# The prologue of the running streams' stage rebuilt, and the first norm done by thirds

## The chip, the cores and the metric

The kernel runs on one core of a Trainium2 chip. A core has a matrix engine (TensorE, PE in the profile), a vector engine (VectorE, DVE), an activation engine (ScalarE, ACT), a general engine (GpSimd, POOL) and a queue engine (SyncE, SP) that issues most transfers. Each engine works through its own instructions in order. The metric is the device time of one execution in microseconds, the median of several runs. Lower is better.

## The reference, cut to what matters

One layer of a streaming encoder is computed for two groups at once: one new stream of 16 + 1024 rows, and 8 running streams of 16 new rows each with a cache of 272 rows. All numbers are float32.

```python
u = rms_norm(h, g_mix)
q, k, v, z, xbc, dt_raw, gate_logits = split(u @ w_in)
att = stick_breaking(q, k, v)              # new stream: its own keys
                                           # running streams: cached keys, then the new ones
ssd = ssd_mix(xbc, z, dt_raw, ...)         # conv, chunked scan, gated norm per group
merged = gate_att * (att @ w_br_att) + gate_ssd * (ssd @ w_br_ssd)
h = h + merged @ w_out
u = rms_norm(h, g_ffn)
h = h + (silu(gate) * val) @ w_down        # gate, val = split(causal_dwconv(u @ w_up))

def stick_breaking(q, k, v):               # per head; reach: key before query
    z = q @ k.T * 64 ** -0.5
    beta = where(reach, sigmoid(z), 0)
    w = beta * (product over later keys of (1 - beta))
    return w @ v
```

Outputs are the final rows of both groups and the new keys, values and states.

## The kernel before, in words

Precision: every large product is done three times, on a high part and a low part of each operand. `split` makes them: a cast on ScalarE (L97) and a subtraction on VectorE (L98). Weights are loaded and split in `weights` (L104 to L106); `mm3` issues the products of one output tile, high by high (L115), low by high (L118), high by low (L119), for each of 8 blocks of the inner dimension. One output block of 128 columns is three tiles of rows (384, 384 and 386 or 400), so 72 matmuls.

Stages in order of the program (`body`):

1. `norm_in`: the rows come in 10 blocks (`x`, L238), handled in three thirds of 3, 3 and 4 blocks. For each block ScalarE squares and sums (L241), takes a root (L242), VectorE makes the reciprocal and refines it (L244, L174 to L177), builds a diagonal (L248), and TensorE spreads it over partitions into `rb` (L249). TensorE transposes the rows (`tp`, L135), ScalarE copies them to `xt` (L264), and VectorE scales them (`un`, L270), after which `split` writes the normalized input `u`, kept in the pool `slotA`. `xt` also goes out to `s_xT` (L276).
2. `phase_ssd`: the state-space part of all four groups.
3. `phase_att`: 16 heads of the new stream. A head loads its keys, queries and values, makes scores (`z`, L721 and L724), a sigmoid (L684), the running product by a scan on VectorE (L688, L690), transposes (`wT`), splits, and the value products (`o`, L745, L746, L753) in two halves `g` of four row blocks. Between the heads stand fill blocks: the remaining q, k, v projections and 16 gate blocks (`gate`, L672, stored by L673). `paced` takes fill blocks from a list; each of a block's three tiles is ordered behind a mark, one of the score matmuls of the heads.
4. `phase_smp`: first `first_queries` (L763 to L802), the first two rows of the new stream for all heads, a small computation that borrows the buffers `Ksh`, `Vsh` and `last`; then `sample_att`, the running streams' attention, 8 streams in two halves of 8 heads each; then `norm_rows` (L926 to L931), which turns the sums of squares of the state-space part (`s_ss`) into factors (`s_rs`). `sample_att` begins with a prologue: queries `qhs`, `qls` (L810), new keys into `kxh`, `kxl` beside the 16 last cached ones (16 loads, L815), the cached rows themselves (16 loads, L821), transposed and split, and the diagonal query tiles `qdh`, `qdl` (L832). In the loop each half loads cached keys and values (`ck`, L856, L858), copies the last keys into `Ksh`, `Ksl` on GpSimd (L862), and does scores (L881 to L885), sigmoid, scan, transposes, and value products (L904 to L906). The output collects in `aout` and is stored once at the end (L918). Six gate blocks are paced by this loop.
5. `phase_merge`: `RESERVE` = 3 gate blocks come first, then `br_ssd`, whose moving operands `ssd_operands` makes: a factor row `rB` (L938), then per block a load `yt` (L941), a multiplication (L943), and the high and low part (L944, L945). Operands 0 to 7 go to the pool `slotB`, 8 to 15 to `slotA`, which is free once the gates no longer read `u`.
6. `phase_ffn`.

What sets the order: a planner orders the instructions of each engine ahead of time by its own estimate of their durations and by the order of the program; at run time each engine keeps that order. Pools open and close like a stack, and a pool opened after another has closed takes its bytes; a tile on such bytes waits for the old tiles that it overlaps, not for the whole stage. Within a stage the order in which pools are named sets which old tile lies under which new one.

## Time and profile before

| | |
|---|---|
| median of 3 runs | 2992.92 us (2991.86 to 2997.25) |
| the profiled execution, its own time | 2993.68 us |
| its span | 2991.6 us |
| PE busy | 2915.2 us, 97% of the span |
| DVE, ACT, POOL busy | 1711.6, 1263.0, 610.3 us |
| first norm | about 0 to 65 us |
| last head ends, running streams begin | about 1445 to 1490 us |
| running streams end, merge begins | about 1645 to 1740 us |

The page lists engines by busy time. A row of the groups reads: line, engine, operation, tile written from tiles read, shapes, count, then busy time and mean duration in ns, then the idle time before it and what ended it. In a row in order of time the first number is the start, the second the duration in us, and the brackets hold the idle time before it and the releaser. The granted clock is that of TensorE, 1.00 being full speed.

### The profile page before, as it was taken

How to read it: one execution, taken by the hardware profiler on the slowest of the kernel's cores; microseconds unless marked ns; L12 is line 12 of the kernel's file. 1: busy time of each engine (PE TensorE's matmuls, PEld its weight loads, DVE VectorE, ACT ScalarE, POOL GpSimd, SP SyncE). 2: the span in 40 equal slices, each digit the busy share in tenths (PEclk: the TensorE clock that was granted, in tenths of full speed). 3: DMA queues.
4: the chain of work that ended last, by engine and by line, in shares of the span. 5: the costliest groups of instructions: out<-in, count | busy, mean ns of one | idle time of the engine just before them, and what ended most of it. 6: DMA issues, size and time to landing. Idle time of an engine off the chain costs nothing. (4 is left out here: it accounts for less than half of the span.)

```text
span 2991.6 us, 45527 instructions
## 1 busy us (share of the span) xinstructions
PE 2915.2 (97%) x17399; PEld 2766.0 (92%) x17399; DVE 1711.6 (57%) x2625; ACT 1263.0 (42%) x2630; POOL 610.3 (20%) x964
## 2 busy tenths in 40 slices
PE   7999999999999999999799899999999999999998
PEld 5998988989889999999789899999999999999998
DVE  6457666576657778777544431446755454545447
ACT  6345454454445455444344310214534242424245
POOL 0023142231322233333233000003201010101013
PEclk9999999999999999999899999999999999999999
DMA  5435355353575555543444643546211111111113
GB/s 187 115 86 157 112 149 147 99 151 108 161 220 145 166 134 144 145 129 98 101 133 131 191 146 98 159 108 185 65 51 44 39 42 43 44 44 37 43 44 120
DMA packets 445496, 338.44 MB, mean 113 GB/s; under 512 B 43991, under 2 KB 421155, under 8 KB 445279
## 3 DMA queue, kind: packets, MB, share of 16 engines
q1 hardware_dynamic: 444063, 333.77, 39.2%
q8 instruction: 137, 2.24, 0.3%
q10 hardware_dynamic: 1216, 1.77, 0.2%
q14 instruction: 80, 0.66, 0.1%
HBM read 244.31 MB, written 91.15 MB: 112 GB/s over the span
## 5 line engine op out<-in xcount | busy, mean ns | idle before, releaser
L115 PE MATMUL mm<-sh,wh 128*128 128x384 f32 (+3 forms) x2520 | 868.3, 346 | 10.3 <-ACT sh L944 5.2
L118 PE MATMUL mm<-sl,wh 128*128 128x384 f32 (+3 forms) x2520 | 869.9, 345 | 1.4 <-DVE sl L98 1.1
L119 PE MATMUL mm<-sh,wl 128*128 128x384 f32 (+3 forms) x2520 | 864.7, 343 | 0.0
L115 PEld LDWEIGHTS mm<-sh,wh 128*128 128x128 f32 (+1 forms) x2520 | 474.5, 188 | 23.6 <-ACT sh L944 5.8
L118 PEld LDWEIGHTS mm<-sl,wh 128*128 128x128 f32 (+1 forms) x2520 | 474.9, 188 | 15.6 <-issue 10.3
L119 PEld LDWEIGHTS mm<-sh,wl 128*128 128x128 f32 (+1 forms) x2520 | 474.9, 188 | 9.4 <-issue 7.8
L115 PE MATMUL mm<-ph,wh 128*128 128x386 f32 x1248 | 424.7, 340 | 0.7 <-DVE st L1041 0.7
L118 PE MATMUL mm<-pl,wh 128*128 128x386 f32 x1248 | 424.9, 340 | 0.0
L106 DVE TENSOR_TENSOR wl<-wf,wh 128x1024 fp32r<-128x1024 f32 (+2 forms) x205 | 253.4, 1237 | 297.5 <-ACT wh L105 281.2
L119 PE MATMUL mm<-ph,wl 128*128 128x386 f32 x1248 | 422.7, 339 | 0.2 <-DVE wl L106 0.2
L105 ACT CAST wh<-wf 128x1024 fp32r<-128x1024 f32 (+2 forms) x205 | 212.5, 1037 | 480.4 <-PE mm L118 455.8
L1153 DVE SCALAR_TENSOR_TENSOR acc<-fx,cwf,acc 128x384 f32<-128x384 f32 (+1 forms) x352 | 170.8, 515 | 155.5 <-ACT acc L1151 151.7
L115 PEld LDWEIGHTS mm<-ph,wh 128*128 128x128 f32 x1248 | 236.3, 189 | 1.6 <-DVE st L1041 1.0
L119 PEld LDWEIGHTS mm<-ph,wl 128*128 128x128 f32 x1248 | 236.2, 189 | 1.1 <-DVE wl L106 0.7
L118 PEld LDWEIGHTS mm<-pl,wh 128*128 128x128 f32 x1248 | 235.2, 188 | 1.7
L688 DVE TENSOR_TENSOR_SCAN keep<-keep 128x144 f32<-128x144 f32 (+7 forms) x128 | 180.0, 1409 | 54.0 <-POOL keep L687 53.4
L115 PE MATMUL mm<-ah,wh 128*128 128x384 f32 x528 | 179.7, 340 | 0.0
L119 PE MATMUL mm<-ah,wl 128*128 128x384 f32 x528 | 179.2, 339 | 0.0
L118 PE MATMUL mm<-al,wh 128*128 128x384 f32 x528 | 179.0, 339 | 0.0
L1080 POOL TENSOR_TENSOR sq<-sq,sq 128x386 f32<-128x386 f32 (+1 forms) x39 | 57.6, 1477 | 463.4 <-ACT sq L1079 455.5
L1178 DVE TENSOR_TENSOR h<-mm,h 128x384 f32<-128x384 f32 x144 | 79.7, 555 | 120.0 <-PE mm L119 119.5
L98 DVE TENSOR_TENSOR wTl<-wT,wTh 128x512 fp32r<-128x512 f32 (+3 forms) x176 | 103.0, 601 | 79.1 <-ACT wTh L97 78.2
(329 smaller groups left out, 4523.9 us busy)
## 6 DMA issues: line engine op xcount, KB each, us to landing
wf<-in_w_in SPq DMA_DIRECT2D x80, 512.0 KB
wf<-in_w_up SPq DMA_DIRECT2D x44, 512.0 KB
t<-s_ac SPq DMA_DIRECT2D x36, 512.0 KB
wf<-in_w_down SPq DMA_DIRECT2D x28, 512.0 KB
wf<-in_w_out SPq DMA_DIRECT2D x24, 512.0 KB
s_y<-x SPq DMA_DIRECT2D x16, 577.0 KB
yt<-s_y SPq DMA_DIRECT2D x16, 577.0 KB
KH<-s_kh SPq DMA_DIRECT2D x32, 260.0 KB
```

The source lines that it names most:

```text
L98: nc.vector.tensor_tensor(out=l, in0=x, in1=h.bitcast(F32), op=ALU.subtract)
L105: nc.scalar.copy(wh, wf)
L106: nc.vector.tensor_tensor(out=wl, in0=wf, in1=wh.bitcast(F32), op=ALU.subtract)
L115: i = nc.tensor.matmul(p, wh[:, k, :], mh[:, c:c + w], start=s, stop=False)
L118: nc.tensor.matmul(p, wh[:, k, :], ml[:, c:c + w], start=False, stop=False)
L119: nc.tensor.matmul(p, wl[:, k, :], mh[:, c:c + w], start=False, stop=e)
L688: nc.vector.tensor_tensor_scan(out=K[:, ::-1], data0=K[:, ::-1], data1=K[:, ::-1], initial=1.0, op0=ALU.mult, op1=ALU.min)
L1080: nc.gpsimd.tensor_tensor(out=acc[:, :w], in0=acc[:, :w], in1=sq, op=ALU.add)
L1153: nc.vector.scalar_tensor_tensor(out=op, in0=src(q), scalar=w(q), in1=op, op0=ALU.mult, op1=ALU.add)
L1178: self.nc.vector.tensor_tensor(out=h, in0=p, in1=h, op=ALU.add)
```

## The change

- The first norm: the sums of squares of a third share one tile; root, reciprocal and refinement are done once per third. Blocks 1 and 2 are loaded by ScalarE's queue. `x` has 6 buffers instead of 5, `xt` holds 2 blocks of columns instead of 4 (so four stores per third instead of two), `rB` has 1 buffer, `un` 3. For two of eight column blocks GpSimd does both halves of the split.
- The attention pools: the heads' tiles get one name for even and one for odd heads with one buffer each (two before under one name), and the pools of both attention stages, and of the fill and row tiles, are opened in another order.
- `first_queries` is called ahead of the last head, and takes its buffers from the pool `cache`, which is opened after the second head.
- The cached rows 256 to 271 of all streams are copied into a scratch tensor `s_ck` after the second head, and loaded from it by two loads. New keys come by two loads into their own tiles; the loop copies the two pieces of 16 keys separately.
- `norm_rows` is called ahead of `sample_att`.
- After the last head one more gate block is taken from the list, ordered behind the last score mark and behind the first value product of each half of the last head. `RESERVE` is 2 instead of 3. The running streams keep six gate blocks.

The diff, cut to its core:

```diff
-RESERVE = 3
+RESERVE = 2
...
+        self.s_ck = dr([TS, 1024], 's_ck')
...
             for p0, p1, c0 in ((0, 3, 0), (3, 6, 384), (6, 10, 768)):
                 xn, o = [], 0
                 rb = self.tile(ps, [128, 512], F32, 'rb', bufs=1)
+                np_ = p1 - p0
+                s = self.tile(sp, [128, 2, 4], F32, 'ss')
+                if p1 == 10:
+                    nc.gpsimd.memset(s[:, 0, 0:np_], 1.0)
                 for i in range(p0, p1):
                     n = sizes[i]
-                    x = self.tile(sp, [128, D], F32, 'x', bufs=5)
+                    x = self.tile(sp, [128, D], F32, 'x', bufs=6)
                     for r, e, src in rows[i]:
-                        nc.sync.dma_start(x[r:e], src)
-                    s = self.tile(sp, [128, 2], F32, 'ss', bufs=4)
+                        (nc.scalar if i in (1, 2) else nc.sync).dma_start(x[r:e], src)
                     sq = self.tile(ps, [128, D], F32, 'sq', bufs=1)
-                    nc.scalar.activation(sq[:n], x[:n], AF.Square, accum_out=s[:n, 0:1])
-                    root = nc.scalar.activation(s[:n, 1:2], s[:n, 0:1], AF.Sqrt, bias=self.eps[:n], scale=1.0 / D)
-                    r = self.tile(sp, [128, 1], F32, 'rs', bufs=4)
-                    nc.vector.reciprocal(r[:n], s[:n, 1:2])
-                    self.refine(sp, r[:n], s[:n, 0:1], 1.0 / D)
+                    nc.scalar.activation(sq[:n], x[:n], AF.Square, accum_out=s[:n, 0, i - p0:i - p0 + 1])
+                    xn.append((x, n))
+                root = nc.scalar.activation(s[:, 1, :np_], s[:, 0, :np_], AF.Sqrt, bias=self.eps, scale=1.0 / D)
+                r = self.tile(sp, [128, 4], F32, 'rs')[:, :np_]
+                nc.vector.reciprocal(r, s[:, 1, :np_])
+                self.refine(sp, r, s[:, 0, :np_], 1.0 / D)
+                for i, (x, n) in enumerate(xn):
...
-                    nc.vector.tensor_scalar(out=dg[:n, :n], in0=self.ident[:n, :n], scalar1=r[:n], scalar2=None, op0=ALU.mult)
+                    nc.vector.tensor_scalar(out=dg[:n, :n], in0=self.ident[:n, :n], scalar1=r[:n, i:i + 1], scalar2=None,
+                                            op0=ALU.mult)
                     nc.tensor.matmul(rb[:, o:o + n], self.ones[:n], dg[:n, :n], start=True, stop=True)
-                    xn.append((x, n))
                     o += n
...
-                xt = [self.tile(sp, [128, 4, 400], F32, 'xt', bufs=3) for _ in range(2)]
+                xt = [self.tile(sp, [128, 2, 400], F32, 'xt', bufs=5) for _ in range(4)]
...
-                    nc.scalar.copy(xt[k // 4][:, k % 4, :w], p[:, :w])
-                rB = self.tile(sp, [128, 400], F32, 'rB', bufs=2)
+                    nc.scalar.copy(xt[k // 2][:, k % 2, :w], p[:, :w])
+                rB = self.tile(sp, [128, 400], F32, 'rB', bufs=1)
...
                 for k in range(8):
-                    y = self.tile(sp, [128, 400], F32, 'un', bufs=2)[:, :w]
-                    nc.vector.scalar_tensor_tensor(out=y, in0=xt[k // 4][:, k % 4, :w], scalar=gT[:, k:k + 1], in1=rB[:, :w],
+                    y = self.tile(sp, [128, 400], F32, 'un', bufs=3)[:, :w]
+                    nc.vector.scalar_tensor_tensor(out=y, in0=xt[k // 2][:, k % 2, :w], scalar=gT[:, k:k + 1], in1=rB[:, :w],
                                                    op0=ALU.mult, op1=ALU.mult)
                     uh, ul = self.u[k]
-                    self.split(uh[:, c0:c0 + w], ul[:, c0:c0 + w], y)
-                    if k % 4 == 3:
-                        q = k // 4
-                        nc.sync.dma_start(self.s_xT[512 * q:512 * q + 512, c0 + z - T0:c0 + w - T0]
+                    uh, ul = uh[:, c0:c0 + w], ul[:, c0:c0 + w]
+                    if k in (2, 5):
+                        nc.gpsimd.tensor_copy(uh, y)
+                        nc.gpsimd.tensor_tensor(out=ul, in0=y, in1=uh.bitcast(F32), op=ALU.subtract)
+                    else:
+                        self.split(uh, ul, y)
+                    if k % 2 == 1:
+                        q = k // 2
+                        nc.sync.dma_start(self.s_xT[256 * q:256 * q + 256, c0 + z - T0:c0 + w - T0]
                                           .rearrange("(i p) t -> p i t", p=128), xt[q][:, :, z:w])
...
-        KH, KL = (self.tile(ap, [128, TP], F32R, n) for n in ('KH', 'KL'))
-        QS = self.tile(ap, [128, TP - T0], F32R, 'QS')
-        VV = self.tile(ap, [128, 9, 128], F32R, 'VV')
+        KH, KL = (self.tile(ap, [128, TP], F32R, f'{n}{h % 2}', bufs=1) for n in ('KH', 'KL'))
+        QS = self.tile(ap, [128, TP - T0], F32R, f'QS{h % 2}', bufs=1)
+        VV = self.tile(ap, [128, 9, 128], F32R, f'VV{h % 2}', bufs=1)
...
-                nc.tensor.matmul(po[:, lo:], VV[:, j, :], wh[:, lo:], start=(j == 0), stop=False)
+                mm = nc.tensor.matmul(po[:, lo:], VV[:, j, :], wh[:, lo:], start=(j == 0), stop=False)
+                if j == 0:
+                    self.pv_marks = [mm] if g == 0 else self.pv_marks + [mm]
...
-        x = self.tile(ap, [128, 4, 288], F32R, 'Ksh').bitcast(F32).rearrange("p a b -> p (a b)")[:, :288]
-        x = x.rearrange("p (i j t) -> p i j t", i=2, j=8)
+        x, v, Q = (self.tile(self.ckp, [128, 2, 512], F32, 'ck').rearrange("p a b -> p (a b)") for _ in range(3))
+        x = x[:, :288].rearrange("p (i j t) -> p i j t", i=2, j=8)
...
-        v = self.tile(ap, [128, 2, 512], F32R, 'Vsh').bitcast(F32)[:16].rearrange("p a (j c) -> p (a j) c", c=128)
+        v = v[:16].rearrange("p (j c) -> p j c", c=128)
...
-        Q = self.tile(ap, [128, 512], F32, 'last', bufs=2)[:, :256].rearrange("p (j c) -> p j c", c=32)
+        Q = Q[:, :256].rearrange("p (j c) -> p j c", c=32)
...
-        ps = self.tile(pa, [128, 512], F32, 'z')
+        ps = self.tile(pa, [128, 512], F32, 'z', bufs=2)
...
-        po = self.tile(pa, [128, 512], F32, 'o')
+        po = self.tile(pa, [128, 512], F32, 'o', bufs=2)
...
-        kx = [self.tile(ap, [128, 8, NB, 32], F32R, n, bufs=1) for n in ('kxh', 'kxl')]
-        for j in range(8):
-            for t, src in zip(kx, (self.s_kh, self.s_kl)):
-                nc.sync.dma_start(t[:, j, :, 16:32].bitcast(F32),
-                                  src[128 * j:128 * j + 128, TP:T].rearrange("p (b t) -> p b t", t=16))
+        kc, kn = ([self.tile(ap, [128, 8, TS], F32R, n + x, bufs=1) for x in 'hl'] for n in ('kc', 'kn'))
+        for t, src in zip(kn, (self.s_kh, self.s_kl)):
+            nc.sync.dma_start(t.bitcast(F32), src[:, TP:T].rearrange("(j p) t -> p j t", p=128))
         for hf in range(2):
             lk = self.tile(ap, [128, 512], F32, 'last', bufs=2)
-            ck = a['cache_k'][0].rearrange("b s h d -> b s (h d)")
-            for b in range(NB):
-                nc.sync.dma_start(lk[16 * b:16 * b + 16], ck[b, 256:272, 512 * hf:512 * hf + 512])
+            nc.sync.dma_start(lk, self.s_ck[:, 512 * hf:512 * hf + 512])
...
-            v = pk.rearrange("p (j b s) -> p j b s", j=4, s=16)
-            h, l = (t[:, 4 * hf:4 * hf + 4, :, 0:16] for t in kx)
-            for j in range(4):
-                self.split(h[:, j], l[:, j], v[:, j])
+            self.split(*(t[:, 4 * hf:4 * hf + 4] for t in kc), pk.rearrange("p (j s) -> p j s", j=4))
...
-                    nc.gpsimd.tensor_copy(K[:, :, 256:288], kx[x][:, 4 * hf:4 * hf + 4, b].bitcast(F32))
+                    for i, k in enumerate((kc, kn)):
+                        nc.gpsimd.tensor_copy(K[:, :, 256 + 16 * i:272 + 16 * i],
+                                              k[x][:, 4 * hf:4 * hf + 4, 16 * b:16 * b + 16].bitcast(F32))
...
             self.ap = {n: self.pool(c1, "att_" + n, 2) for n in (
-                'wTh', 'wTl', 'wf32', 'att', 'vf', 'KH', 'KL', 'QS', 'VV', 'keep', *(f'beta{i}' for i in range(8)))}
+                'KH0', 'KL0', 'QS0', 'VV0', 'vf', *(f'beta{i}' for i in range(8)), 'KH1', 'KL1', 'QS1', 'VV1', 'keep',
+                'wTh', 'wTl', 'wf32', 'att', 'fb', 'fw', 'fo')}
...
                 for e in range(2):
+                    if p == 7 and e == 1:
+                        self.first_queries()
                     marks += self.head(2 * p + e, v[:, :, 64 * e:64 * e + 64])
...
-        self.ckp = self.pool(right, "cache", 4, side='right')
+                        self.ckp = self.pool(right, "cache", 4, side='right')
+                        self.nc.sync.dma_start(self.s_ck.rearrange("(b s) c -> b s c", s=16),
+                                               self.a['cache_k'][0, :, 256:272].rearrange("b s h d -> b s (h d)"))
+            self.fill.pop(0)([marks[-1]] + self.pv_marks)
...
         with ExitStack() as c2:
-            mp = self.stp = self.pool(c2, "mixst", 3)
+
             self.ap = {n: self.pool(c2, "smpa_" + n, 2) for n in (
-                'aout', 'od', 'wTh', 'wTl', 'keep', 'beta', 'v', 'r', 'newton', 'qdh0', 'qhs', 'qls', 'kxh', 'kxl',
-                'last', 'V3h', 'V3l', 'qdl0', 'qdh1', 'qdl1', 'Ksh', 'Ksl', 'Vsh', 'Vsl',
-                'w30', 'w31', 'fb', 'fw', 'fo')}
+                'last', 'qdh0', 'qdl0', 'qdh1', 'qdl1', 'qhs', 'qls', 'knh', 'knl', 'kch', 'kcl', 'Ksh', 'Ksl', 'V3h', 'V3l',
+                'v', 'r', 'newton', 'beta', 'keep', 'Vsh', 'Vsl', 'w30', 'w31', 'wTh', 'wTl', 'od', 'aout')}
+            self.stp = self.pool(c2, "mixst", 3)
             self.pa = self.pool(c2, "smp_ps", 1, space=PSUM)
             rest, self.fill = self.fill[len(self.fill) - RESERVE:], self.fill[:len(self.fill) - RESERVE]
-            self.first_queries()
+            self.norm_rows(self.ap)
             self.sample_att(3 * len(self.fill) / 16)
-            self.norm_rows(self.ap)
...
             with ExitStack() as c1:
+                k.rowp = k.pool(c1, "rows", 2)
                 k.stp = k.pool(c1, "fill", 7)
-                k.rowp = k.pool(c1, "rows", 2)
```

## The prediction

> **What bounds the kernel now.** I read the page first, then a table of stretches, then the TensorE (PE) order of time where the table shows holes, then the queues that release PE there.
>
> ```profile
> span 2991.6 us, 45527 instructions
> ...
> PE 2915.2 (97%) x17399; PEld 2766.0 (92%) x17399; DVE 1711.6 (57%) x2625; ACT 1263.0 (42%) x2630; POOL 610.3 (20%) x964
> ```
>
> PE is busy for 97% of the span, so the bound is matmul work and the question is where PE stands still or runs slowly. The change adds and removes almost no matmul work, so I count in "lost time": the length of a stretch less busy time times granted clock. The columns are stretch, its length, busy time of PE, weight loads, DVE, ACT, POOL, the clock, the DMA share and GB/s.
>
> ```profile
> 6.00:20.00 14.00, 10.22 (x43) 7.31 (x43) 9.38 (x39) 12.09 (x29) 0.38 (x2) 1.00 0.96 311
> 20.00:65.00 45.00, 38.41 (x190) 27.52 (x191) 29.74 (x79) 29.84 (x70) 0.00 (x0) 0.89 0.44 150
> 1445.00:1465.00 20.00, 13.17 (x59) 9.58 (x58) 11.71 (x15) 6.25 (x14) 4.59 (x8) 0.74 0.89 111
> 1465.00:1490.00 25.00, 17.03 (x93) 16.09 (x92) 8.10 (x23) 10.27 (x23) 7.68 (x17) 0.66 0.56 154
> 1645.00:1660.00 15.00, 10.06 (x49) 6.81 (x49) 5.26 (x10) 6.78 (x13) 1.96 (x3) 1.00 0.24 69
> 1700.00:1712.00 12.00, 7.92 (x30) 7.09 (x30) 6.61 (x5) 3.84 (x4) 0.00 (x0) 0.72 0.70 224
> 1712.00:1740.00 28.00, 26.58 (x151) 26.26 (x150) 18.61 (x14) 9.35 (x8) 0.00 (x0) 1.00 0.69 224
> 1750.00:1800.00 50.00, 50.00 (x287) 50.00 (x286) 10.88 (x15) 5.25 (x5) 0.00 (x0) 1.00 0.42 127
> ```
>
> The first norm (6 to 65) loses 14 - 10.22 = 3.8 and 45 - 38.41 x 0.89 = 10.8, together 14.6 us. The handover from the last head to the running streams (1445 to 1490) loses 20 - 13.17 x 0.74 = 10.3 and 25 - 17.03 x 0.66 = 13.8, together 24.1 us, the largest hole of the run. The streams' last two halves lose 4.9 us (1645 to 1660), and the merge loses 12 - 7.92 x 0.72 = 6.3 and 1.4, together 7.7 us. The last row gives the price of a dense matmul, 50 / 287 = 0.174 us, so a gate block of 72 matmuls is 12.5 us of cover and one of its three tiles 4.2 us.
>
> What ends the waits of the handover, on PE and on DVE:
>
> ```profile
> 1452.38 0.69 PE L135 MATMUL wT<-ident,beta 128*128 128x128 f32 x2 [2.24 <-DVE beta L690]
> ...
> 1460.21 0.50 PE L746 MATMUL o<-wTl,VV 128*128 128x512 f32 x1 [2.18 <-DVE wTl L98]
> ...
> 1467.70 0.63 PE L135 MATMUL pk<-ident,last 128*128 128x128 f32 x4 [1.91 <-DMA last<-in_cache_k]
> 1473.37 0.21 PE L135 MATMUL wT<-ident,fb 32*16 32x32 f32 x1 [5.04 <-DVE fb L791]
> 1473.84 3.62 PE L798 MATMUL o<-fw,Vsh 16*128 16x32 f32 x16 [0.26 <-ACT fw L795]
> ```
> ```profile
> 1446.39 1.31 DVE L106 TENSOR_TENSOR wl<-wf,wh 128x1024 fp32r<-128x1024 f32 x1
> ...
> 1459.25 0.31 DVE L770 TENSOR_TENSOR Ksh<-Ksh 128x144 f32<-128x144 f32 x1 [4.46 <-DMA Ksh<-s_kl]
> ```
>
> The 2.24 us is the last head's own scan. The 2.18 us is not: DVE stood 4.46 us at the first addition of the first two queries (L770), which sits in its in-order queue ahead of the head's split, until their loads had landed. The 5.04 us is the same small computation again, its product on DVE.
>
> **Part 1, the handover.** The loads that stood in that queue:
>
> ```profile
> 1445.62 0.66 SPq L815 DMA_DIRECT2D kxh<-s_kh  x1
> ...
> 1461.06 0.82 SPq L815 DMA_DIRECT2D kxl<-s_kl  x1
> ```
> ```profile
> kxh<-s_kh SPq DMA_DIRECT2D x8, 64.0 KB
> kxl<-s_kl SPq DMA_DIRECT2D x8, 64.0 KB
> last<-in_cache_k SPq DMA_DIRECT2D x16, 32.0 KB
> ```
>
> Sixteen loads of new keys hold SP's queue from 1445.62 to 1461.88, 16.3 us, in which the DMA engines are 89% busy for only 111 GB/s: they move runs of 16 floats. The sixteen loads of cached rows follow. The change makes four loads of these 32, plus one copy into a scratch tensor issued far ahead, after the second head. The new key tiles, query tiles and diagonal tiles now lie on bytes of the even head's tiles and of the row tiles, which are free before the last head ends; the small query computation, with its loads, moves in front of the last head and past SP's loads of that head. I therefore expect the 1.91, 5.04 and 0.26 us and, through DVE, the 2.18 us to go: 9.4 us of idle time. The slow clock in these 45 us is 13.17 x 0.26 + 17.03 x 0.34 = 9.2 us more and follows from the gaps. What else is late is the last head's chain, where one more gate block now stands: its tiles may come after the last head's score product and after the first value products of its two halves, so two of three tiles (8.4 us) fall where the 2.24 us and its neighbours are.
>
> Bounds for what remains of the 24.1 us: at best 3 us (the 2.24 us and small ones), gain 21; at worst the whole slow clock stays and only the 9.4 us go, gain 9. I take 8 us left, gain 16, nearer to the good end, since 12.5 us of cover stands against 24.1 - 9.4 - 9.2 = 5.5 us of other idle time.
>
> The moved computation keeps its PE work (17 small products) and adds its DVE and POOL steps to the last head; a wait there is covered by gate tiles, and if that cover fails it costs the 4.46 us again. The norm of rows, moved before the streams' loop, brings an ACT table load into the last head's tail:
>
> ```profile
> 1470.38 1.28 ACT L927 ACT_TABLE_LOAD   x1 [1.75 <-DMA v<-s_ss]
> ```
>
> It is in the kernel already, so it costs nothing new unless a split of the last head stands behind it, then 1.3 us. In the loop POOL makes four copies per half where it made two:
>
> ```profile
> L862 POOL CAST Ksh<-kxh 128x128 fp32r<-128x128 f32 x16 | 4.8, 302 | 6.3 <-ACT kxh L97 5.4 <-PE z L885 0.9
> L583 POOL TENSOR_TENSOR sq<-sq,zf 128x384 f32<-128x384 f32 x24 | 24.9, 1035 | 46.0 <-ACT zf L582 46.0
> ```
>
> At 302 ns or less for half the elements that is at most 2 x 16 x 0.3 = 9.7 us more of POOL work in 180 us, hidden under PE's dense gates. Zero.
>
> **Part 2, the merge.** It starts with two gates instead of three: 12.5 us of cover gone. What was covered is the chain of operands, load, multiply, split:
>
> ```profile
> 1645.35 0.29 PE L885 MATMUL z<-Ksh,qdl 128*128 128x288 f32 x1
> ```
> ```profile
> 1660.54 0.37 SPq L918 DMA_DIRECT2D s_att<-aout  x1
> 1661.01 0.52 SPq L938 DMA_DIRECT2D rB<-s_rs  x1
> 1666.16 0.81 SPq L941 DMA_DIRECT2D yt<-s_y  x2
> ```
> ```profile
> 1670.41 1.36 DVE L943 TENSOR_TENSOR yt<-yt,rB 128x1154 f32<-128x1154 f32 x1 [14.64 <-DMA yt<-s_y]
> ...
> 1745.00 1.36 DVE L943 TENSOR_TENSOR yt<-yt,rB 128x1154 f32<-128x1154 f32 x1 [0.16 <-DMA yt<-s_y]
> ```
>
> Adding up the pools by their sizes, the first `yt` buffer (bytes 4,616 to 9,232 of the region) lies on the old `aout` (4,800 to 8,896), so its load had to wait until the store of `aout`, issued at 1660.54, had landed: 1666.16. In the new order `aout` is near the end, and under `rB` and `yt` lie `last` and the four diagonal tiles, last read by the score product at 1645.35. The chain can begin up to 20 us earlier; its second pair still needs the first `sl` slots, which lie on `V3h` and `V3l` until the last value product near 1657, so about 15 us are real. The chain runs from 1670 to 1746, about 10 us a pair. Ending 15 us earlier against 12.5 us less cover is 2.5 us of gain; bounds are +12.5 us (chain not earlier) and -7.7 us (hole closed). I take -1.5.
>
> **Part 3, the first norm.** Its rows:
>
> ```profile
> L97 ACT CAST sh<-un 128x384 fp32r<-128x384 f32 (+1 forms) x24 | 12.5, 523 | 2.2 <-DVE un L270 2.0
> ...
> L98 DVE TENSOR_TENSOR sl<-un,sh 128x384 fp32r<-128x384 f32 (+1 forms) x24 | 13.4, 557 | 4.2 <-ACT sh L97 3.9
> ...
> L242 ACT ACTIVATE ss<-ss,eps 128x1 f32<-128x1 f32 (+1 forms) x10 | 3.1, 312 | 0.1
> ...
> L244 DVE RECIPROCAL rs<-ss 128x1 f32<-128x1 f32 (+1 forms) x10 | 1.6, 158 | 8.8 <-ACT ss L242 8.8
> ```
>
> ACT loses seven of ten roots (7 x 0.312 = 2.2 us) and six casts (6 x 0.523 = 3.1 us), 5.3 us; DVE loses seven times five small steps (some 0.158 us each, 5.5 us) and six subtractions (3.3 us). POOL, idle there, takes six pairs: the subtraction at about the 1.035 us of L583, the copy between 0.3 and 1.0 us. A pair thus takes 1.3 to 2.0 us where cast and subtraction took 1.08, and the third's reciprocals wait for its last square. ACT was busy for 12.09 of 14 us in the first stretch, so it is the limit there, but later not. Bounds: -5.3 to +1; I take -2.5. The two loads on ACT's queue and the sixth `x` buffer I cost at nothing, since the DMA share is already 0.96 then; at the worst two issues delay ACT inside the +1.
>
> **Sum.** -16 - 1.5 - 2.5 = -20 us. The profiled execution took 2993.68 us for a span of 2991.6, 0.8 us over the median of 2992.92; 2993.7 - 20 = 2973.7, against the median 2972.9. I predict 2973.
>
> **The rivals.**
>
> *The hole moves.* SP is in order; if `rB` and `yt` stay behind the store of `aout` as now, only its landing (1660.5 to 1666.2, 5.6 us) is won. Merge 12.5 - 5.6 = +6.9: -16 + 6.9 - 2.5 = -11.6, 2982 us. For it: `rB` was issued right behind that store although its bytes were not under `aout`.
>
> *POOL and DVE take turns in the norm.* The same POOL subtraction took 1.26 and 1.71 us, the longer beside a DVE step with two SBUF operands:
>
> ```profile
> 1466.60 1.26 POOL L876 TENSOR_TENSOR Vsl<-ck,Vsh 128x512 fp32r<-128x512 f32 x1
> ...
> 1479.06 1.71 POOL L876 TENSOR_TENSOR Vsl<-ck,Vsh 128x512 fp32r<-128x512 f32 x1 [3.20 <-ACT Vsh L874]
> ```
> ```profile
> 1478.94 0.69 DVE L876 TENSOR_TENSOR Vsl<-ck,Vsh 128x512 fp32r<-128x512 f32 x1 [4.67 <-ACT Vsh L874]
> ```
>
> If all six pairs (up to 12 us of POOL) held up DVE, less the 8.8 us that it saves, the start would go +3 instead of -2.5: 2978.5 us. The Trainium skill, "SBUF - State Buffer", section "SBUF: two separate sides", states such a rule: a GpSimd operation and a DVE operation with two SBUF inputs exclude each other for a whole instruction. The 0.45 us between the two rows agrees with it.
>
> *The cover is taken from where it was needed (slower).* If the last head's chain on DVE and ACT, not PE, sets the handover, the gate's own weight split on DVE (1.31 us) and on ACT its cast and three sigmoids lengthen it, and the tiles gain nothing:
>
> ```profile
> 1443.26 1.06 ACT L105 CAST wh<-wf 128x1024 fp32r<-128x1024 f32 x1
> 1444.21 0.49 ACT L672 ACTIVATE st<-mm 128x386 f32<-128x386 f32 x1
> ```
>
> That is 1.31 + 1.06 + 3 x 0.49 = +3.8. The merge meanwhile opens by the whole 12.5 us and restarts at slow clock (7.92 x 0.28 = 2.2). Against it stand only 9.4 and 2.5: 12.5 + 2.2 + 3.8 - 9.4 - 2.5 = +6.6, 3000 us. It decides once the handover gives back less than the merge loses. Against it: the handover's PE idles in gaps of 2 us and more that any ready matmul can fill.
>
> *The change does not do what it says.* The bytes still collide, and the first keys wait as before; then only the norm and the 2.18 us remain: -4.7, 2989 us.
>
> **How the numbers follow.** Forecast 0.55 (its own range 2960 to 2983, from 21 + 5.3 + 7.7 = 34 us of gain down to 10), hole moves 0.17, turns 0.10, slower 0.10, no effect 0.08. The range 2960 to 2988 leaves out the slower case, the one without effect and slivers. About 6 us, 0.2%, is what a measurement tells from no change: faster 0.55 + 0.10 + 0.15 of the second = 0.80, same 0.02 + 0.08 = 0.10, slower 0.10.
>
> **What would show it.** Right: in the 45 us around the end of the last head the clock stays above 0.9 and lost time is under 10 us; no DVE wait of 4 us on loads of the first queries; the first streams' score product follows the last head's value products at once; `yt` is issued before the store of `aout`; the root group counts 3. Wrong: three gate tiles in a handover that still runs at half clock, or PE idle for over 10 us between the last reserved gate and the second half of the branch product.

## The result, and the profile after

The changed kernel takes 2969.88 us (median of 4 runs, 2969.4 to 2971.83); the kernel before, timed beside it, takes 2993.04 us (4 runs, 2991.86 to 2997.25). The ratio is 0.9914 with a 95% interval of 0.9902 to 0.9926, so the change saves 23 us. The forecast was 20 us and 2973. The profiled execution has a span of 2967.9 us where the kernel before had 2991.6, a difference of 23.7 us, which the traces have to explain. One execution of a later kernel (the first norm of before, measured again) took 4940 us at a granted clock of 0.66 and is left out of its median.

The page of the changed kernel: its span, and the busy time of each engine.

```profile
span 2967.9 us, 45503 instructions
...
PE 2909.5 (98%) x17399; PEld 2764.3 (93%) x17399; DVE 1711.7 (58%) x2578; ACT 1259.3 (42%) x2611; POOL 626.7 (21%) x1009
```

The number of matmuls is the same, so the gain is again a matter of where PE stands still or runs slowly. The table of stretches of the changed kernel, with the columns that the prediction named. The two middle rows are the 25 us up to the end of the last head and the 20 us behind it, now later, since a gate block and the first queries are done inside.

```profile
6.00:20.00 14.00, 9.36 (x39) 7.55 (x39) 3.40 (x12) 10.84 (x24) 0.44 (x3) 1.00 0.95 296
20.00:65.00 45.00, 38.79 (x195) 28.65 (x196) 35.66 (x67) 27.83 (x64) 12.80 (x12) 0.89 0.50 171
1447.50:1472.50 25.00, 24.64 (x155) 22.51 (x156) 15.61 (x23) 12.25 (x24) 2.05 (x4) 1.00 0.39 109
1472.50:1492.50 20.00, 15.13 (x74) 14.09 (x74) 7.45 (x11) 7.35 (x12) 11.61 (x33) 0.74 0.56 174
1700.00:1712.00 12.00, 10.87 (x62) 10.55 (x61) 8.18 (x8) 3.64 (x4) 0.00 (x0) 1.00 0.61 188
1712.00:1740.00 28.00, 27.02 (x153) 26.37 (x152) 17.50 (x17) 7.14 (x6) 0.00 (x0) 1.00 0.62 196
```

In the last head PE now loses 25 - 24.64 = 0.4 us, and in the 20 us behind it 20 - 15.13 x 0.74 = 8.8 us, 9.2 us in 45 us where 24.1 us were lost. The whole slow clock that is left lies behind the head, not in it. The hole of the merge (1700 to 1740) has shrunk from 7.7 to 2.1 us. The first norm shows 4.6 + 10.5 = 15.1 us where there were 14.6.

What is left behind the last head shows in the order of time on PE: the last value products, the transposes of the cached rows (`last`), those of the first cache tile (`ck`), and the first score product of the running streams.

```profile
1472.08 0.54 PE L766 MATMUL o<-wf,VV 128*128 128x144 f32 x4
1472.46 1.07 PE L135 MATMUL pk<-ident,last 128*128 128x128 f32 x8
1476.52 1.95 PE L135 MATMUL pk<-ident,ck 128*128 128x128 f32 x8 [2.98 <-DVE kcl L98]
1479.01 1.12 PE L135 MATMUL pk<-ident,ck 128*128 128x128 f32 x4 [0.55 <-DVE Ksl L98]
1481.47 0.61 PE L889 MATMUL z<-Ksh,qdh 128*128 128x288 f32 x1 [1.34 <-POOL Ksh L869]
```

The two transposed tiles of cached rows hold both PSUM buffers named `pk`, so the next transposes wait 2.98 us for their split, and the score product starts 9.0 us after the first transpose. ACT, at that moment, does something else first:

```profile
1473.14 1.99 ACT L882 CAST Vsh<-ck 128x1024 fp32r<-128x1024 f32 x2
1475.15 1.07 ACT L97 CAST kch<-pk 128x512 fp32r<-128x512 f32 x2
```

The merge's chain of operands, on SP's queue and as the groups that work on `yt` (minimum, median and maximum of one in ns, then the first and the last start); first the changed kernel, then the same group before the change:

```profile
1635.46 0.32 SPq L946 DMA_DIRECT2D rB<-s_rs  x1
1638.98 0.79 SPq L949 DMA_DIRECT2D yt<-s_y  x2
...
1655.54 0.37 SPq L926 DMA_DIRECT2D s_att<-aout  x1
```
```profile
L952 ACT ACTIVATE sh<-yt,gv x16: 1248/1262/1268, 1655.5 to 1726.7; 128x1154 fp32r<-128x1154 f32 x16
L953 DVE SCALAR_TENSOR_TENSOR sl<-yt,gv,sh x16: 1412/1421/1425, 1656.8 to 1728.0; 128x1154 fp32r<-128x1154 f32 x16
```
```profile
L945 DVE SCALAR_TENSOR_TENSOR sl<-yt,gv,sh x16: 1412/1420/1423, 1674.0 to 1747.7; 128x1154 fp32r<-128x1154 f32 x16
```

`yt` is loaded 16.6 us ahead of the store of `aout`, where it stood behind it. The first split moves from 1674.0 to 1656.8, the last from 1747.7 to 1728.0. The store has not left the chain altogether: the second split on DVE still waits for its landing.

```profile
1660.49 1.43 DVE L953 SCALAR_TENSOR_TENSOR sl<-yt,gv,sh 128x1154 fp32r<-128x1154 f32 x1 [2.24 <-DMA s_att<-aout]
```

To see where 23.7 us went, I cut the run at the same landmarks in every kernel and added up lost time (length less busy time of PE times its clock, in stretches of 5 us). The busy time that is left differs between these kernels, which do the same work, by up to 5 us (by 6.5 us over all fourteen profiles), so a difference of 2 us in one row alone says little. The columns behind "after" are a second profile of the changed kernel and five of the experiments below.

| lost, us | before | after | after, 2nd | gate back | queries back | loads back | `aout` first | keys early |
|---|---|---|---|---|---|---|---|---|
| 0 to 65, first norm | 20.6 | 20.5 | 19.9 | 18.3 | 19.1 | 19.2 | 20.2 | 18.1 |
| 65 to 1435 | 16.6 | 19.1 | 17.0 | 19.2 | 18.0 | 20.5 | 18.8 | 18.7 |
| 1435 to the last head's end | 9.7 | 0.5 | 2.0 | 11.5 | 1.4 | 0.4 | 2.1 | 0.7 |
| 35 us behind it | 14.8 | 8.7 | 8.3 | 5.4 | 9.9 | 8.4 | 9.3 | 5.0 |
| streams' loop | 6.2 | 1.4 | 1.4 | 3.1 | 1.5 | 4.9 | 4.0 | 4.0 |
| streams' last halves | 4.9 | 6.7 | 6.4 | 5.4 | 5.8 | 8.5 | 3.8 | 4.1 |
| merge to the branch's end | 8.3 | 2.1 | 1.4 | 2.9 | 3.4 | 5.9 | 11.6 | 4.7 |
| rest | 11.4 | 11.2 | 11.0 | 10.3 | 11.3 | 11.9 | 12.4 | 11.5 |
| sum | 92.4 | 70.2 | 67.4 | 76.1 | 70.5 | 79.6 | 82.1 | 66.7 |

The handover (the rows from 1435 to 35 us behind the last head: 24.4 us before, 9.2 after) gave 15.2 us, the merge 6.2 and the streams' loop 4.8; the last halves took 1.8 and the stretch from 65 to 1435 took 2.5. The sums differ by 22.2 us; the other 1.5 us of the 23.7 lie in busy time.

### The profile page after: what moved, and what is told of

Its sections match the earlier page's. It is cut to its first block, busy times and chain, and to the rows that moved or that the text cites. A ratio compares the mean times of both kernels' runs of the same rounds, so it can differ in the third digit from the quotient of the medians.

```text
span 2967.9 us, 45503 instructions
## 1 busy us (share of the span) xinstructions
PE 2909.5 (98%) x17399; PEld 2764.3 (93%) x17399; DVE 1711.7 (58%) x2578; ACT 1259.3 (42%) x2611; POOL 626.7 (21%) x1009
## 3 DMA queue, kind: packets, MB, share of 16 engines
q8 instruction: 137, 2.24, 0.3%
## 4 chain that ended last, share of the span: by engine, by line
PE 84%; DMA 5%; DVE 3%; ACT 2%; issue 1%; POOL 1%; SPq 1%; DVEq 0%; ACTq 0%; POOLq 0%
PE mm L115 23%; PE mm L118 22%; PE mm L119 22%; PE wT L135 2%; DMA yt<-s_y 1%; PE yd L501 1%; PE z L732 1%; PE z L735 1%; PE st L484 1%; PE px L135 1%; PE o L759 1%; DMA zf<-s_z 1%; PE o L756 1%; PE yo L510 1%; DMA wf<-in_w_out 1%
## 5 line engine op out<-in xcount | busy, mean ns | idle before, releaser
L118 PEld LDWEIGHTS mm<-sl,wh 128*128 128x128 f32 (+1 forms) x2520 | 474.9, 188 | 18.7 <-issue 10.3
```

The lines of the kernel that those rows point to most:

```text
L118: nc.tensor.matmul(p, wh[:, k, :], ml[:, c:c + w], start=False, stop=False)
```

## The experiments

**The gate behind the last head goes back to the merge.** Three gates are held in reserve, as before; all else is the changed kernel.

```
-RESERVE = 2
+RESERVE = 3
-            self.fill.pop(0)([marks[-1]] + self.pv_marks)
```

> The changed kernel, but no gate block is taken from the list behind the last head, and three gate blocks are kept for the merge again. Theory (the gate's tiles fill the waits of the last head): the stretch from 1440 us to the end of the last head, which lost 9.7 us before and 0.4 us after, loses 6 to 9 us again, the merge gains back at most its 3.2 us; about 2974 to 2977 us. Rival (the hole only moved, the gain comes from the prologue): within 1.5 us of 2970.

Measured: 2976.65 us (2973.53 to 2980.15), ratio to the kernel before 0.9939 (0.9924 to 0.9954), 6.8 us above the changed kernel. The 25 us up to the end of the last head, and PE's longest wait in them:

```profile
1444.25:1469.25 25.00, 16.34 (x89) 12.59 (x89) 15.54 (x22) 9.81 (x20) 9.59 (x17) 0.80 0.41 104
```
```profile
1458.59 0.69 PE L135 MATMUL wT<-ident,beta 128*128 128x128 f32 x2 [4.63 <-DVE beta L701]
```

Without the gate the head loses 25 - 16.34 x 0.80 = 11.9 us, against 0.4. The last head's own scan (`beta`) makes PE wait 4.63 us, twice the 2.24 us of the kernel before: the loads no longer stand in its way, and yet the head loses more than before the change (11.5 against 9.7 in the table). So it is the gate's matmuls that fill the head. Behind the head this kernel loses less than the changed one (5.4 against 8.7), so of the 11.0 us in the head 7.7 are left for the handover as a whole. It costs the merge little that they are gone from there: 2.9 us lost with three gates, 2.1 with two.

**The first two queries go back behind the last head**, into the running streams' tiles, at the head of their stage.

```
-                    if p == 7 and e == 1:
-                        self.first_queries()
...
+            self.first_queries()
             self.norm_rows(self.ap)
```

> The changed kernel, but the first two queries are computed at the head of the streams' stage again, in tiles of that stage. Theory (DVE's wait for their loads and the wait for their product, 2.2 and 5.0 us of PE idle before, return, partly under the moved gate): plus 4 to 8 us, 2974 to 2978 us. Rival (the moved gate covers them): within 1.5 us of 2970.

Measured: 2969.71 us (2968.43 to 2970.87), ratio 0.9917 (0.9900 to 0.9933): no difference to the changed kernel. DVE again stands at the addition for the first queries, and PE waits behind the head for the cached rows:

```profile
DVE Ksh L783 <- DMA Ksh<-s_kl: 2.5, 1, 2.5
```
```profile
PE pk L135 <- DMA last<-s_ck: 6.2, 1, 6.2
```

The DVE wait that the forecast counted as a loss is here again (2.5 us where it was 4.46), and the last head loses 1.4 us all the same: the gate stands over it. The 6.2 us behind the head take the place of the 2.98 and 1.34 us, and cost 1.2 us more there. The move of the first queries is worth nothing that the times can tell, once the gate lies in the last head; the forecast of 4 to 8 us fell.

**The 32 small loads and the interleaved key tile come back**, with one POOL copy per part of the keys, the split of the cached rows in four pieces per half, and no scratch tensor.

```
-            nc.sync.dma_start(lk, self.s_ck[:, 512 * hf:512 * hf + 512])
+            for b in range(NB):
+                nc.sync.dma_start(lk[16 * b:16 * b + 16], ck[b, 256:272, 512 * hf:512 * hf + 512])
...
+        for j in range(8):
+            for t, src in zip(kx, (self.s_kh, self.s_kl)):
+                nc.sync.dma_start(t[:, j, :, 16:32].bitcast(F32), ...)
```

> The changed kernel, but with the 16 loads of new keys and 16 of cached rows of before, and one copy per key part in the loop. Theory (the queue of 32 small loads delays the prologue): plus 5 to 10 us, 2975 to 2980 us. Rival (what counts is that the tiles lie on bytes that are free early; the loads are issued before the last head ends and are hidden): within 2 us of 2970.

Measured: 2975.77 us (2973.71 to 2978.13), ratio 0.9936 (0.9921 to 0.9951), 5.9 us slower, at the limit of what a measurement tells, and not where the forecast put it:

```profile
1476.43 1.88 PE L135 MATMUL pk<-ident,ck 128*128 128x128 f32 x8 [4.60 <-DVE kxl L98]
```
```profile
L957 DVE SCALAR_TENSOR_TENSOR sl<-yt,gv,sh x16: 1412/1420/1423, 1660.5 to 1735.2; 128x1154 fp32r<-128x1154 f32 x16
```

In the last head and the 35 us behind it this kernel loses 8.7 us, as the changed one does (9.2): the split `kxl` takes the place of `kcl`. The spans of the two profiles differ by 7.9 us (2975.8 against 2967.9), and what is lost more lies in the loop, the last halves and the merge (3.5, 1.8 and 3.8 us), whose chain ends at 1735.2 instead of 1728.0. The loop's part says little, since the next kernel, which has the few loads, also loses more in it (4.0 us against 1.4). Which of the differences does the rest, the loads, the interleaved tile, the split in pieces or the copies, was not separated.

**`aout` and the mixer's staging lie first in the streams' region again**, under `rB` and `yt`.

```
-                'last', 'qdh0', ... 'wTl', 'od', 'aout')}
-            self.stp = self.pool(c2, "mixst", 3)
+            self.stp = self.pool(c2, "mixst", 3)
+                'aout', 'last', 'qdh0', ... 'wTl', 'od')}
```

> The changed kernel, but in the streams' stage the pool of gate results and the output tile lie first in the region again, as before. Theory (the merge's first operand loads wait for the store of the output): the first operand load comes behind that store, some 15 to 20 us later, and the merge, with one gate less than before, loses 10 to 15 us instead of 3.2: 2977 to 2982 us. Rival (the chain of operands is not what the merge waits for): within 2 us of 2970.

Measured: 2979.41 us (2977.01 to 2981.98), ratio 0.9948 (0.9933 to 0.9963), 9.5 us slower. The merge loses as much more (11.6 us against 2.1); the other rows of the table, from -2.9 to +2.6, add up to 2.4 us. SP's queue and DVE's first operand:

```profile
1656.41 0.37 SPq L926 DMA_DIRECT2D s_att<-aout  x1
...
1662.60 0.81 SPq L949 DMA_DIRECT2D yt<-s_y  x2
```
```profile
1667.10 1.36 DVE L951 TENSOR_TENSOR yt<-yt,rB 128x1154 f32<-128x1154 f32 x1 [14.52 <-DMA yt<-s_y]
```

The load is again issued 6.2 us behind the store (SP's wait for the store's landing is 5.2 us of them), and DVE stands 14.52 us, as in the kernel before (14.64). This is the wait that the new order of the pools removes, and the 9.5 us are its price here.

**The last heads' pools in the old order**, with the key tiles of even and odd heads side by side.

```
-  'KH0', 'KL0', 'QS0', 'VV0', 'vf', beta0..7, 'KH1', 'KL1', 'QS1', 'VV1', 'keep', 'wTh', ...
+  'wTh', 'wTl', 'wf32', 'att', 'vf', 'KH0', 'KH1', 'KL0', 'KL1', ... 'keep', beta0..7, 'fb', 'fw', 'fo'
```

> The changed kernel, but the pools of the heads' tiles stand in the old order again (split tiles first, the scan tiles of the eight row blocks last; the separate names for even and odd heads stay). Theory (the prologue can only start early because its tiles lie on the even head's bytes): queries and new keys then lie on bytes that the last head uses to its end, the first streams' score product comes later, and the prologue loses 12 to 16 us instead of 8.7: 2973 to 2978 us. Rival (the prologue waits for the end of the last head on TensorE anyway, whatever the bytes): within 1.5 us of 2970.

Measured: 2971.42 us (2971.01 to 2975.43), ratio 0.9922 (0.9907 to 0.9937), 1.5 us above the changed kernel, which a measurement does not tell from no change. In its profile the 35 us behind the head lose 10.7 us, where the two of the changed kernel lose 8.7 and 8.3, and not the 12 to 16 us of the forecast. That the streams' first tiles lie on bytes that are free before the last head ends was a condition in the forecast; by itself it can't be told from nothing here.

**The first norm of before** in the changed kernel (roots one by one, the old numbers of buffers, all loads on SP's queue, no POOL), measured twice, the second time beside the changed kernel itself.

```
-                root = nc.scalar.activation(s[:, 1, :np_], s[:, 0, :np_], AF.Sqrt, ...)
+                    root = nc.scalar.activation(s[:n, 1:2], s[:n, 0:1], AF.Sqrt, ...)
...
-                    if k in (2, 5):  (POOL's copy and subtraction)
+                    self.split(uh[:, c0:c0 + w], ul[:, c0:c0 + w], y)
```

> The changed kernel with the first norm of before, block by block. Theory from the two traces (the norm by thirds gave nothing: 20.6 us lost before 65 us without it and 20.5 with it): within 1 us of 2970. Rival (the forecast's 2.5 us are there and were lost again at the start of the attention): 2972 to 2973 us, with 2 to 3 us more lost up to 850 us.

> The changed kernel with the first norm of before, a second time and beside the changed kernel itself. Theory of the forecast: the norm by thirds is worth 2.5 us, so this is 2972 to 2974. Rival, from the traces up to 65 us (20.6 us lost before, 20.5 after): it is worth nothing, and this is 2969 to 2971.

> The changed kernel itself, a second time, as the measure of what two profiles of one kernel differ by. Theory: the handover (last head and 35 us behind it) and the merge are steady, 9 to 10 us and 2 to 3 us lost, while the streams' loop (1.4 us in the first profile) and the 25 us before the first head (4.2) wander by 2 to 3 us, as they did in kernels in which nothing of them was changed (loop 1.5 to 3.8, before the first head 1.0 to 2.7). Rival: the loop again loses under 2 us, and what it gained on the kernel before (6.2) is the change's. Time 2970 in both cases.

Measured: first 2973.68 us (2971.36 to 2977.75), ratio 0.9928 (0.9913 to 0.9943); then 2973.22 us (2966.18 to 2977.56), a ratio of 0.9921 (0.9908 to 0.9934), beside 2967.37 us (2964.89 to 2969.67) and 0.9908 (0.9895 to 0.9921) for the changed kernel at the same time. Both differences of the ratios are 0.0013 to 0.0014, some 4 us, and both pairs of intervals overlap. By the traces the first 65 us lose 22.5 and 30.6 us with the old norm; with the new one, in the eight profiles of kernels that do not touch it, 18.1 to 20.5. The highest of the old was:

```profile
20.00:65.00 45.00, 34.59 (x153) 25.11 (x153) 27.85 (x77) 27.22 (x64) 0.00 (x0) 0.70 0.50 172
```

A good part of it is slow clock (0.70, against 0.89 in the first profile of either kernel), so the size wanders. Both differences point the way of the forecast's 2.5 us, but neither is told apart from no change, and the size is not settled: nearly nothing by the first profiles before and after (20.6 and 20.5), 4 us by the times.

The second profile of the changed kernel answers another question too, whether the loop's small loss is chance:

```profile
1505.00:1635.80 130.80, 129.44 (x804) 122.88 (x804) 57.74 (x99) 60.50 (x121) 51.86 (x134) 1.00 0.43 137
```

It loses 130.80 - 129.44 = 1.36 us, to a hundredth what the first profile lost. My theory that the loop wanders between profiles of one kernel is not borne out by these two: inside one kernel the loss repeats. Small edits elsewhere do move it, though (3.1 us with the gate back, 4.0 with the keys early), so its gain of 4.8 us can be put down to no single part.

**No POOL in the norm**, and then **all loads of the norm on SP's queue besides**.

```
-                    if k in (2, 5):
+                    if False:
...
-                        (nc.scalar if i in (1, 2) else nc.sync).dma_start(x[r:e], src)
+                        nc.sync.dma_start(x[r:e], src)
```

> The changed kernel, but GpSimd does none of the splits of the first norm. Theory (GpSimd and DVE hold each other up): the scaling step on DVE returns from 741 to about 617 ns and the subtraction from 630 to about 557 ns, and the time falls by 1 to 3 us although ScalarE gets 3.1 us of casts back: 2967 to 2969 us. Rival (ScalarE is the limit of the norm): the same DVE durations, but plus 1 to 3 us.

> As the last, and all row blocks are loaded by SP's queue again, as before. Theory (two queues make the first block arrive late): the first transposes, which came at 6.3 us before and at 9.2 us after, come at 6 to 7 us again, and another 1 to 3 us are won over the kernel without GpSimd's splits. Rival (the arrival of the third block decides, not the first): no difference to it beyond 0.5 us.

Measured: 2969.34 us (2967.87 to 2969.71) without POOL and 2969.99 us (2967.33 to 2972.26) with SP's loads too, ratios 0.9911 (0.9896 to 0.9926) and 0.9911 (0.9895 to 0.9928): both as the changed kernel; neither of the two gains of 1 to 3 us came. The norm's groups of the changed kernel, then of the one without POOL:

```profile
L276 DVE SCALAR_TENSOR_TENSOR un<-xt,gT,rB 128x384 f32<-128x384 f32 (+1 forms) x24 | 16.9, 741 | 0.3
...
L98 DVE TENSOR_TENSOR sl<-un,sh 128x384 fp32r<-128x384 f32 (+1 forms) x18 | 11.2, 630 | 1.2 <-ACT sh L97 1.0
...
L282 POOL TENSOR_TENSOR sl<-un,sh 128x384 fp32r<-128x384 f32 (+1 forms) x6 | 6.9, 1156 | 0.5
L281 POOL CAST sh<-un 128x384 fp32r<-128x384 f32 (+1 forms) x6 | 5.9, 977 | 26.4 <-DVE un L276 24.1 <-DVE rs L178 2.3
```
```profile
L276 DVE SCALAR_TENSOR_TENSOR un<-xt,gT,rB 128x384 f32<-128x384 f32 (+1 forms) x24 | 14.3, 620 | 0.1
...
L98 DVE TENSOR_TENSOR sl<-un,sh 128x384 fp32r<-128x384 f32 (+1 forms) x24 | 13.2, 558 | 2.1 <-ACT sh L97 2.0
```

Beside POOL's pairs DVE's steps take 741 and 630 ns instead of 620 and 558: 24 x 0.121 + 18 x 0.072 = 4.2 us more, against 6 x 0.558 = 3.3 us of subtractions taken off DVE. The delay is not spread evenly: the medians hardly move (622 and 556 ns beside POOL, 618 and 556 without), while the longest steps go from 635 to 1359 ns and from 577 to 1460. So a few steps are held up, by as much as 0.7 to 0.9 us, beside POOL operations of 1.0 and 1.2 us. On DVE the delay takes back what POOL's help saves, and by the times the help comes to nothing. The loads differ in their order of arrival: PE's first products on `x` in the changed kernel (in the one without POOL they start at 9.18 us too) and in the one with one queue.

```profile
9.18 2.15 PE L135 MATMUL tp<-ident,x 128*128 128x128 f32 x9 [3.61 <-DMA x<-in_x_prompt]
```
```profile
6.60 0.87 PE L135 MATMUL tp<-ident,x 128*128 128x128 f32 x3 [3.14 <-DMA x<-in_x_prompt]
```

With two queues the first block can be used 2.6 us later, but three blocks at once; the time is the same.

**The cached rows' keys done early.** They are transposed and split beside the third pair of heads and stored to a scratch tensor, so that the streams load them as they load the new keys; and the same without POOL in the norm.

```
+                    if p == 2 and e == 0:
+                        self.cached_keys()
...
-            pk = self.tile(pa, [128, 512], F32, 'pk', bufs=2)
-            ... (transposes and split of lk)
+        for t, src in zip(kc, (self.s_kch, self.s_kcl)):
+            nc.sync.dma_start(t.bitcast(F32), src.rearrange("(j p) t -> p j t", p=128))
```

> The transposes and the split of the cached rows' keys are done beside the third pair of heads, with the 16 cache tiles' bytes, and stored to a scratch tensor; the running streams load the two halves as they load the new keys. Theory: what is left of the handover (8.7 us lost in the 35 us behind the last head, 3.9 of it slow clock) is one chain: the two transposed tiles hold both PSUM buffers until a cast that stands behind a 2.0 us cast of values and a subtraction are done (PE waits 2.98 us), and the first score product waits 1.3 us for copies of the result. Without it 3 to 5 us are lost there and the time is 2965 to 2967. Rival: the first half's own tiles (the split of its keys, the subtraction of its values on POOL, 2.5 us for two) end no sooner, the wait changes its name, and the time stays within 1.5 us of 2970.

> The same with all splits of the first norm on ACT and DVE, none on POOL. Theory: POOL's share in the norm is worth nothing or costs up to 1 us (2969.34 without it against 2969.88 with it, in different calls), so this is the same as the kernel with only the keys moved, or 1 us less. Rival, from the norm's forecast: POOL's six splits save 1 to 2 us, and this is that much slower than the kernel with only the keys moved.

Measured: 2969.26 us (2967.79 to 2973.23), ratio 0.9917 (0.9904 to 0.9929), and 2967.41 us (2966.14 to 2969.84), ratio 0.9909 (0.9897 to 0.9922), beside 2967.37 us and 0.9908 for the changed kernel: no gain in either. The 20 us behind the last head, PE's order in them, ACT's order, and the merge's chain of the first of the two:

```profile
1472.50:1492.50 20.00, 16.61 (x94) 15.92 (x93) 7.51 (x13) 6.89 (x12) 10.52 (x31) 0.91 0.59 182
```
```profile
1472.38 1.07 PE L135 MATMUL pk<-ident,ck 128*128 128x128 f32 x8
1476.68 1.25 PE L135 MATMUL pk<-ident,ck 128*128 128x128 f32 x8 [3.23 <-DVE Ksl L98]
1478.10 0.61 PE L899 MATMUL z<-Ksh,qdh 128*128 128x288 f32 x1 [0.16 <-POOL qdh L883]
```
```profile
1473.30 1.99 ACT L892 CAST Vsh<-ck 128x1024 fp32r<-128x1024 f32 x2
1475.32 1.07 ACT L97 CAST Ksh<-pk 128x512 fp32r<-128x512 f32 x2
```
```profile
L963 DVE SCALAR_TENSOR_TENSOR sl<-yt,gv,sh x16: 1414/1420/1423, 1653.1 to 1727.7; 128x1154 fp32r<-128x1154 f32 x16
```

Here the theory and the rival are each half right. The score product starts 3.4 us earlier, the clock is 0.91 instead of 0.74 and 20 - 16.61 x 0.91 = 4.9 us are lost behind the head, against 8.8. But the longest wait only changes its name, to 3.23 us for the first half's own split, because ACT still does 1.99 us of the values' cast ahead of it. And the gain does not reach the end. The chain of the merge starts 3.7 us earlier than in the first profile of the changed kernel (1653.1 against 1656.8) and ends with it (1727.7 against 1728.0); in the second profile of the changed kernel, whose last head ends 2.5 us earlier than in the first, it runs from 1653.6 to 1724.3.

That end is the common figure of all these runs. In all twelve profiles with two gates in the merge (the changed kernel twice, and every kernel here but the one with three), the span less the start of the last of these splits is 1238.9 to 1240.6 us, while the spans go from 2963.2 to 2980.3: for instance 2967.9 - 1728.0 = 1239.9, 2980.3 - 1739.8 = 1240.5 with `aout` first, and here 2967.3 - 1727.7 = 1239.6. With three gates it is 1243.9 before the change and 2973.7 - 1723.4 = 1250.3 in the changed kernel with its gate put back. So with two gates the time of the run is read off the end of this chain, and, but for these 1.7 us, all differences between these kernels have arisen before it. The constant by itself does not make the chain their cause, since the work behind it is the same in all of them; that PE does wait for its steps is seen in the merge's rows (1.8 us for `sh` and 0.3 for `sl` in the first profile of the changed kernel). From first to last split the chain took 74.6 us here, and 71.2 and 70.7 in the two profiles of the changed kernel. DVE's waits for loads of `yt` add up to 27.8 us here, and to 24.6 and 24.2 there, which is nearly the difference; why these loads came later stays open.

## Why the prediction was right, and where it was not

**The sum.** -20 was forecast, -23 measured, inside the forecast's own range; the likeliest case came. Its three terms did not all come for the reasons given, and that the total came so near is in part luck. Against the forecast, by the first profiles, the handover gave 0.8 us less, the merge 4.7 more, the norm 2.4 less, the loop 4.8 more, all other rows together 4.1 less, and busy time 1.5 more: misses that add up to only 3.7 us.

**The handover, -16.** By the landmarks it gave 15.2 us, and 9.2 us are left where I took 8: the size is right. The mark of a clock above 0.9 with under 10 us lost is met barely, (24.64 x 1.00 + 15.13 x 0.74) / (24.64 + 15.13) = 0.90. The working, though, added 9.4 us of waits that go with the loads and the first queries, and then slow clock that follows. The experiments contradict this first step. In the table's two rows of the handover, where the kernel before lost 24.4 us, the kernel with the first queries back behind the head loses 11.3 and the one with the 32 loads back 8.7, against 9.2 and 10.4 in the two profiles of the changed kernel. With the gate taken out they lose 16.9 us, so some 7.7 of the 15.2 are the gate's. The other 7.5 us come from the rest taken together; no experiment took out the gate and another part at once, so their shares stay open. That the sum met 15.2 us by this working is luck. I had called the gate cover for what was left; it is cover for the waits that I had counted as removed, too.

**What is late next** was missing. The streams' score product was to follow the last head's value products at once; it came 9.0 us after the transposes began, behind the cached rows' split. The wait for the cached rows' loads (1.91 us) did go, and the split behind it was what came next. The rows for this stood in the trace of before: two `pk` buffers, and the transposes of `last` ahead of those of `ck`.

**The merge, -1.5** with bounds +12.5 and -7.7, gave 6.2. The mechanism is the one I gave (the store of `aout` no longer under `yt`, and then the slots that the last value products hold), and the kernel with `aout` first prices it at 9.5 us. Of those slots I had named only a part. The trace shows the first `sh` right behind ACT's last copy into `aout`, and the second split waiting 2.24 us for the landing of the store of `aout`, so the start of the chain hangs on `aout` too and not only on the last value products. The size was off: I took 15 us of lead against 12.5 us of cover, and the last split came 19.7 us earlier, 17.2 of which its first one already had. 19.7 - 12.5 = 7.2 us, which is near the 6.2 us of the hole. I had counted the second pair's wait from the old kernel's time of the last value product, 1657, without the streams themselves ending earlier: ACT copied the last `aout` at 1655.09 and the first `sh` started at 1655.5. The terms of handover and merge were added as if they were apart, while the second's lead depends on the first's gain.

**The first norm, -2.5.** The times say some 4 us with intervals that overlap, the traces up to 65 us between nothing and 10. The parts of the working fared unevenly: the roots and reciprocals went as counted, three of each:

```profile
L247 ACT ACTIVATE ss<-ss,eps 128x3 f32<-128x3 f32 (+1 forms) x3 | 1.0, 336 | 0.0
...
L249 DVE RECIPROCAL rs<-ss 128x3 f32<-128x3 f32 (+1 forms) x3 | 0.5, 168 | 13.3 <-ACT ss L247 13.3
```

The six pairs on POOL were to save ACT and DVE 3.1 and 3.3 us; taking them away leaves the time as it was (2969.34 against 2969.88 us). The pair takes 1.156 + 0.977 = 2.1 us, a little above my upper end of 2.0.

**The loop was costed at zero**, for POOL's copies, and they are hidden indeed. But the loop lost 6.2 us before and 1.4 after. Of the 6.2, 3.4 us were PE's wait for loads of cached keys; the waits of PE in the loop, before and after, with their total, number and longest:

```profile
PE pk L135 <- DMA ck<-in_cache_k: 3.4, 2, 2.2
```
```profile
PE pk L135 <- DMA ck<-in_cache_k: 0.2, 1, 0.2
```

The forecast followed SP's queue to the first score product and no further. But the 32 loads do not explain it. With them back, the same wait stands at

```profile
PE pk L135 <- DMA ck<-in_cache_k: 1.0, 1, 1.0
```

and in kernels that have the few loads it goes from nothing (first queries back) over 1.3 us (`aout` first) to 2.4 us (keys early, no POOL in the norm). What moved these 3.2 us stays open.

**The rivals.** "The hole moves" fell: `rB` and `yt` were issued ahead of the store, and only the second split still waits for its landing. "POOL and DVE take turns" was right on the mechanism and wrong on its price: DVE's steps do grow by 4.2 us, not by up to 12, and what it loses there POOL's help gives back. By the rule of the Trainium skill ("SBUF - State Buffer", section "SBUF: two separate sides") a GpSimd operation and a DVE step with two SBUF inputs exclude each other; the 741 and 630 ns beside POOL against 620 and 558 without it agree with it, and the few long steps (up to 1359 and 1460 ns, with the medians unmoved) do so more closely. "Cover taken from where it was needed" fell: the head fills instead of growing, and the merge needs the third gate less than the head does. "The change does not do what it says" fell with the rows of SP.

## What to carry to other kernels

Ready matmuls fill a wait of PE whatever it is for, as the gate did here with the scan's and the first queries' waits: before pricing each wait that a change removes, count which of them the moved cover fills anyway, or the same microseconds are counted twice. When two terms of a sum follow each other in time on one chain, work out the date at which the chain starts and ends after the first term, and only then the second; here one late operation (the start of the last split of the merge) gave the end of the run within 2 us in all twelve profiles with two gates in the merge. And where a stall goes, look up the next holder of the same buffers: here two PSUM tiles, and a 2 us cast in front on ACT.

## What the runs showed of the hardware

The granted clock falls to half behind short gaps, and how long it stays there does not follow from the length of the first gap. In the changed kernel the longest gap behind the last head is 2.98 us and the clock over those 20 us is 0.74, which costs 15.13 x 0.26 = 3.9 us beside the 4.9 us of idle time. Read in stretches of 1 us, it is 0.50 there for 10.2 us in all, with gaps of 0.55 and 1.34 us inside. With the keys done early the gap is 3.23 us, nearly alone, and the clock is 0.50 for 3.4 us (0.91 over the 20 us). With the first queries back the gap is 6.2 us, and the clock is 0.50 for 6.8 us from there. That the gaps which follow weigh more than the length of the first one fits these three traces; no run changed the one without the other. All three times are multiples of 3.4 us, and so are those of the kernel before in the handover (10.3 and 17.1 us).

DVE steps that run beside POOL's splits are 20% (741 against 620 ns) and 13% (630 against 558 ns) longer on average, carried by a few steps of up to 1359 and 1460 ns. The profile shows it as longer steps and not as waits: the idle time before the 24 scaling steps is 0.3 us.

Splitting a set of loads over two queues brought the first block 2.6 us later (9.18 against 6.60 us), with no change of the total time (2969.34 against 2969.99 us, both without POOL in the norm).
